# A one-core hybrid encoder step: other SBUF addresses for matmul operands, one block's down products summed over two chunks, and a wider last multiply

## The chip, the cores and the metric

The kernel runs on one core of a Trainium2 chip. The metric is the device time of one execution in microseconds (us). It is quoted as the median of several runs of the same program; one further execution was recorded by the hardware profiler, and all rows below come from that one.

## What is computed

One layer of a streaming encoder for 2048 prompt frames and 32 sample frames, model width 1024. The reference, cut to its steps:

```python
z = rmsnorm(h, g_attn) @ w_in                  # q, k, v of two head groups
oa = diff_attn(qa, ka, va, t5_table, lam)      # 4 heads, two softmax maps each
ob = band_attn(qb, kb, vb, band_table)         # 8 heads, a band of 9 chunks of 64
h = h + concat(subnorm(oa), rmsnorm(ob)) @ w_out
c = rmsnorm(h, g_mlp)
h = h + square(relu(c @ w_up)) @ w_down        # 1024 -> 4096 -> 1024
h = h + sigmoid(h @ w_ple_gate) * (p @ w_ple_proj)
y = rmsnorm(h, g_final)
```

The outputs are y and the new keys and values of both groups, for the prompt and for the sample.

## The kernel before, in words

**Matmuls.** Every fp32 product is made of three fp32r matmuls (mm3, lines 220 to 222): each operand is split into a high part (a rounding copy, on ACT or DVE, line 182 or 184) and a low part (raw minus high, on POOL, lines 167 and 177, or on DVE, line 188). Of a matmul, the *stationary* operand (128 columns) is loaded into the array and the *moving* operand (up to 512 columns) streams past it. A row `ups<-cs,piece 128x256` is a matmul into PSUM tile `ups` with moving operand `cs`, stationary operand `piece`, and 256 moving columns.

**Blocks and stages.** The 2080 frames are four blocks: 0, 1 and 2 of 512 columns, and 3 of 544 (512 prompt and 32 sample frames), which is worked in two sub-blocks of 272 (SUBS, line 36). The stages, in order of time: norm and projections (`vps` values, `qps` queries and keys), in between and after them attention B (`sb`, `tpb`, `ob`) and attention A (`s` scores, `tpp` transposes, `o` output sums), output projections (`ops`), MLP (`ups` up products, `dps` down products), the gate (`gps`, `pps`), and the final norm. A scheduler that works from a timeline model of its own decides in which order the instructions of overlapping stages stand in each engine's queue. Each engine works through its queue in order; all DMAs are issued from SP's queue.

**The MLP of blocks 2 and 3 (mlp7, line 1170).** 16 chunks of 256 hidden units. In each chunk a Strassen-like scheme with seven products of half size replaces eight: seven `prod` calls (line 1198) of 12 matmuls each, 84 `ups` matmuls of 256 columns (block 2) or 272 (block 3). ACT copies (line 1202) and DVE adds (line 1204) empty their PSUM banks, and relu, square and split (lines 1207 to 1210) make two hidden tiles in high and low parts: four tiles `uh`, `ul` in the pool `uh` (`up` in the code), a ring of 20 tiles of 544 columns. The chunk's down products, `downs` (line 1174), run beside the next chunk's up products: 8 groups of 6 matmuls, and after each group one DVE add of the PSUM bank to the residual `h` (line 1193). Weights come in `wr` tiles by DMA and are split into `piece` tiles, a ring of 8 (six slots in pool `wp4`, two in `wx`). While block 2 is in this stage, `cstage` (line 1024) prepares the seven operands of block 3: it draws its `ct` and `cst` tiles from the same ring of 20, stores them to DRAM, and their slots come free when the store has landed.

**Addresses.** A tile lies at the same byte address in each of the 128 partitions. The matter of the change is where a matmul's moving operand starts, taken modulo 256 bytes; it is called the *phase* below. It follows from the tile widths. A tile of 512 or 1024 fp32 columns is a whole number of 256-byte steps; a ring tile of 544 columns is 2176 bytes, 8.5 steps, so that the tiles of that ring start at phase 0 and 128 in turn. The two sub-blocks of 272 columns lie 1088 bytes apart, so that the second starts 64 further on. Pools on the right side of SBUF are stacked below each other, so that what the first of them, `edge` (24 columns, 96 bytes), takes shifts all the others.

**The final norm (final, line 1368).** For block 3 (`end`), per sub-block: DVE makes the reciprocal root (lines 1401 to 1403) and scales h tile 7 (line 1405); tiles 6 and 5 are multiplied by it on POOL, tiles 4 to 0 by five DVE multiplies (line 1413), and each half of the eight tiles is stored by one DMA.

Of the kernel before, what the change touches and what calls it, by code (L numbers as in the profile page):

```python
# [20 lines left out]
P = 128  # L21
# [121 lines left out]


class Kern:
    def __init__(self, tc, a):
        self.tc = tc
        self.nc = tc.nc
        self.a = a
        self.nt = 3  # L150
        self.pieces = None

    def dma(self, dst, src):
# [36 lines left out]
    def wunit(self, src, shape, hi_eng="act", lo_eng="pool", pool=None):  # L190
        nc = self.nc
        if pool is None:
            raw = self.rawp.tile([P] + shape, F32, bufs=2, name="wr")
        else:
            raw = pool.tile([P] + shape, F32, tag="wr0", bufs=4, name="wr0")
        self.dma(raw, src)
        if self.pieces is not None:
            n = shape[0] // 2
            parts = []
            for x in range(2):  # L200
                parts.append(self.piece([n] + shape[1:]))
# [407 lines left out]
    def attn_a_pair(self, g, j, ka, ba, pool, ps_s, ps_t, ps_o, late, first=None):  # L609
# [72 lines left out]
        for c0 in range(0, len(kts), 4):  # L682
# [8 lines left out]
            else:  # L691
# [104 lines left out]
    def attn_b_pair(self, h, j, kt, v, kb, bb, q, t1, pool, ps_s, ps_t, ps_o, step, late):  # L796
# [9 lines left out]
        for qi, t in enumerate(tiles):  # L806
# [37 lines left out]
            def second(qi=qi, nr=nr, kts=kts, held=held, end=t is tiles[-1]):  # L844
                if qi == 0:
                    px.append(pool.tile([P, 6, 2, 256], F32R, tag="p", bufs=2, name="pb"))
                p = px[0]
                e = held[0]
# [65 lines left out]
    def oload(self, b, wk, up, out, r=None):  # L914
# [74 lines left out]
    def cparts(self, b, wk, cs, out, r):  # L989
# [34 lines left out]
    def cstage(self, b, up, out, r):  # L1024
# [6 lines left out]
        def parts(k, *which):  # L1031
            for x, raw in which:
                t = up.tile([P, up.aw], F32R, tag="u", name="cst")[:, :n]
                self.split(t[:, :m], t[:, m:], raw, "act", "dve")
# [3 lines left out]
        for k in range(4):  # L1038
            c = []
            for i in range(2):  # L1040
                tmp = up.tile([P, up.aw], F32, tag="u", name="ct")[:, :n]
                kk = k + 4 * i
# [127 lines left out]
    def mlp7(self, b, hh, box, ops, wk, up, mm, md):  # L1170
        nc = self.nc
        n = BN[b]
        m = n // 2
        def downs(ch, us):
            for dh in range(2):
                wh, wl = self.wunit(self.a["w_down"][2 * ch + dh], [2, 512])
                for d in range(4):
                    for s0, sn in SUBS[b]:
# [75 lines left out]
        for ch in range(DFF // (2 * P)):  # L1254
            if ch > 0:
                w = {}
                drain(weights(ch, w, self.piece))
            us = []
            for f in range(2):
                us.append([up.tile([P, up.aw], F32R, tag="u", name=x)[:, :n] for x in ("uh", "ul")])  # L1260
            r0, r1 = tmp("r0", n), tmp("r1", n)
# [12 lines left out]
            prod(c12, u2, w["s4"], "b22")  # L1274
            square(us[0], r0, "dve")
            next(prev, None)
            prod(c21, u3, w["a22"], "t4")
            square(us[1], r1, "pool")
            drain(prev)
            prev = downs(ch, us)  # L1280
            yield
        drain(prev)

    def hparts(self, b, wk, up, out):
        n, t0 = BN[b], 512 * b
        hH, hL = [[up.tile([P, BLK], F32R, tag="u", name="hu")[:, :n] for k in range(8)] for _ in range(2)]
        out.append((hH, hL))
# [7 lines left out]
    def ptile(self, b, up, wk):  # L1295
        n, t0 = BN[b], 512 * b
        pT = [[up.tile([P, up.aw], F32R, tag="u", name="pT") for _ in range(2)] for _ in range(2)]
        for k in range(2):
            raw = (
                up.tile([P, up.aw], F32, tag="u", name="praw") if wk is None  # L1300
                else wk.tile([P, BLK], F32, tag="tmp", bufs=self.nt, name="praw")
# [5 lines left out]
    def gate(self, b, h, up, act, md, wk=None, made=None, pT=None):  # L1307
# [13 lines left out]
        else:  # L1321
            hH, hL = [[up.tile([P, BLK], F32R, tag="u", name="hu")[:, :n] for k in range(8)] for _ in range(2)]
        if made is None:
            for k in range(8):
                self.split(hH[k], hL[k], h[:, k, :n], "act", "dve" if k % 2 else "pool")
        for dq in range(2):
            ph, pl = self.wunit(a["w_ple_proj"][dq], [2, 512])
            for d4 in range(4):
                d = 4 * dq + d4
                wh, wl = self.wunit(a["w_ple_gate"][d], [8, P])  # L1330
                for s0, sn in SUBS[b]:
# [5 lines left out]
                    sg = (  # L1337
                        up.tile([P, up.aw], F32, tag="u", name="sig") if wk is None
                        else wk.tile([P, BLK], F32, tag="tmp", bufs=self.nt, name="sig")
# [28 lines left out]
    def final(self, b, h, wk, mm):  # L1368
# [22 lines left out]
        for s0, sn in SUBS[b]:  # L1391
# [14 lines left out]
            for k in range(6, -1, -1):  # L1406
                hv = h[:, k, sub]
                if not end:
                    nc.vector.scalar_tensor_tensor(hv, hv, self.g_final[:, k : k + 1], y, op0=ALU.mult, op1=ALU.mult)  # L1409
                elif k in (5, 6):  # L1410
                    self.pool_tt(hv, hv, y, ALU.mult)
                else:
                    nc.vector.tensor_tensor(hv, hv, y, op=ALU.mult)
# [296 lines left out]
```

## Time and profile before

| what | us |
|---|---|
| median of 3 runs | 3025.55 (3023.77 to 3027.49) |
| the profiled execution, its own time | 3025.88 |
| its span, first to last instruction | 3023.8 |
| PE busy (matmuls, their ends modelled) | 2925.0 (97% of the span) |
| DVE, ACT, POOL busy | 1823.2, 1746.1, 1887.1 (60%, 58%, 62%) |
| mean granted TensorE clock | 0.990 of full speed |

Of the profiled execution's time, 2.1 us lie outside its span. The views used are: the page with its summary and its line of 40 slices; the list of waits (engine, line, what it waited for, us in total, times, longest); groups by line and shape (busy us, mean ns of one, idle time before); busy time by windows; and the timeline, whose rows give start, duration, engine, line and instruction. A matmul's duration holds its way through the array, which overlaps the next one's: what a matmul costs in a stream is the distance from start to start, its *pitch*.

### The profile page before, as it was taken

What the parts mean: (1) busy time and instruction counts of PE and PEld (TensorE: products, weight loads), DVE (VectorE), ACT (ScalarE), POOL (GpSimd) and SP (SyncE); (2) the same over time, 40 slices, a digit from 0 to 9 for tenths busy, and PEclk for the clock granted to TensorE, in tenths of its full rate; (3) what the DMA queues carried; (4) which work ended last, traced back from release to release, by engine and by line L of the source; (5) the groups of instructions that cost most, each with busy time, mean ns of one, the idle gap of its engine ahead of it and who ended that gap; (6) DMA issues with size and microseconds to landing.
All of it is one profiled execution on the core that took longest, in us unless ns stands there. A gap on an engine that the chain in (4) does not pass through costs nothing. (4 is left out here: it accounts for less than half of the span.)

```text
span 3023.8 us, 49919 instructions
## 1 busy us (share of the span) xinstructions
PE 2925.0 (97%) x17217; PEld 2576.6 (85%) x17217; DVE 1823.2 (60%) x4217; ACT 1746.1 (58%) x3226; POOL 1887.1 (62%) x2509
## 2 busy tenths in 40 slices
PE   8999999999989999999999999999999999999997
PEld 6798889999877888888888888778788887999997
DVE  5256554676565554667566566445677885677664
ACT  5365554777666665655665655554655455555455
POOL 2568775323465444666655655787688888787774
PEclk9999999999999999999999999999999999999999
DMA  9877867987887453655643543446423446323231
GB/s 311 283 235 237 242 205 220 272 238 223 251 251 219 136 152 105 188 150 168 207 143 124 149 141 111 157 157 209 162 91 134 142 142 239 129 91 119 98 103 54
DMA packets 295204, 528.45 MB, mean 175 GB/s; under 512 B 36316, under 2 KB 159232, under 8 KB 294952
## 3 DMA queue, kind: packets, MB, share of 16 engines
q1 hardware_dynamic: 294952, 525.27, 55.7%
q8 instruction: 136, 2.23, 0.3%
q14 instruction: 116, 0.95, 0.1%
HBM read 424.66 MB, written 104.45 MB: 175 GB/s over the span
## 5 line engine op out<-in xcount | busy, mean ns | idle before, releaser
L177 POOL TENSOR_TENSOR wl<-wr,wh 128x256 fp32r<-128x256 f32 x632 | 472.0, 780 | 246.2 <-ACT wh L182 218.3
L182 ACT ACTIVATE piece<-wr 128x512 fp32r<-128x512 f32 x406 | 245.4, 624 | 290.4 <-PE ups L221 131.2
L177 POOL TENSOR_TENSOR piece<-wr,piece 128x256 fp32r<-128x256 f32 x404 | 338.2, 862 | 93.5 <-ACT piece L182 87.0
L182 ACT ACTIVATE wh<-wr 128x1024 fp32r<-128x1024 f32 x228 | 240.0, 1055 | 200.2 <-PE ups L221 42.6
L167 POOL TENSOR_TENSOR wl<-wr,wh 128x256 fp32r<-128x256 f32 x280 | 216.6, 805 | 202.1 <-ACT wh L182 199.9
L220 PE MATMUL dps<-uh,piece 128*128 128x272 f32 (+1 forms) x768 | 246.7, 325 | 10.3 <-ACT piece L182 6.8
L167 POOL TENSOR_TENSOR piece<-wr,piece 128x256 fp32r<-128x256 f32 x280 | 237.2, 879 | 18.2 <-ACT piece L182 14.9
L222 PE MATMUL dps<-uh,piece 128*128 128x272 f32 (+1 forms) x768 | 247.1, 324 | 1.5 <-POOL piece L167 1.0
L221 PE MATMUL dps<-ul,piece 128*128 128x272 f32 (+1 forms) x768 | 247.0, 323 | 0.1
L221 PE MATMUL ups<-cs,piece 128*128 128x256 f32 (+1 forms) x864 | 244.8, 283 | 0.0
L220 PE MATMUL ups<-cs,piece 128*128 128x256 f32 (+1 forms) x864 | 244.8, 283 | 0.0
L222 PE MATMUL ups<-cs,piece 128*128 128x256 f32 (+1 forms) x864 | 244.7, 284 | 0.0
L220 PE MATMUL qps<-aH,wh 128*128 128x512 f32 (+1 forms) x640 | 227.4, 356 | 5.8 <-DVE ql L502 4.2
L221 PE MATMUL qps<-aL,wh 128*128 128x512 f32 (+1 forms) x640 | 227.2, 355 | 0.0
L222 PE MATMUL qps<-aH,wl 128*128 128x512 f32 (+1 forms) x640 | 226.7, 355 | 0.0
L665 ACT ACTIVATE e<-e,nm 128x128 f32<-128x128 f32 (+16 forms) x136 | 157.2, 1156 | 109.6 <-DVE nm L663 109.1
L1150 DVE TENSOR_TENSOR h<-h,dps 128x512 f32<-128x512 f32 x256 | 173.1, 681 | 69.0 <-PE dps L222 67.8
L1193 DVE TENSOR_TENSOR h<-h,dps 128x272 f32<-128x272 f32 (+1 forms) x384 | 188.8, 513 | 42.3 <-PE dps L222 41.7
L220 PE MATMUL dps<-uh,wh 128*128 128x512 f32 x512 | 204.7, 400 | 5.6 <-DVE h L1150 4.5
L220 PE MATMUL ups<-cH,wh 128*128 128x512 f32 x512 | 202.5, 396 | 0.0
L222 PE MATMUL ups<-cH,wl 128*128 128x512 f32 x512 | 202.3, 395 | 0.0
L221 PE MATMUL ups<-cL,wh 128*128 128x512 f32 x512 | 202.2, 395 | 0.0
(312 smaller groups left out, 9139.7 us busy)
## 6 DMA issues: line engine op xcount, KB each, us to landing
wr<-w_up SPq DMA_DIRECT2D x128, 512.0 KB, 3.5
wr<-w_down SPq DMA_DIRECT2D x128, 512.0 KB, 3.5
q<-qS SPq DMA_DIRECT2D x128, 256.0 KB, 5.2
v<-vSa SPq DMA_DIRECT2D x64, 512.0 KB, 4.6
wr<-w_qk SPq DMA_DIRECT2D x50, 512.0 KB, 5.0
ka<-kS SPq DMA_DIRECT2D x32, 512.0 KB, 7.4
wr<-w_out SPq DMA_DIRECT2D x32, 512.0 KB, 4.5
wr<-w_ple_gate SPq DMA_DIRECT2D x32, 512.0 KB, 4.1
```

Of the source, the lines that this page charges most:

```text
L167: nc.gpsimd.tensor_tensor(out[:, sl], a[:, sl], b[:, sl], op=op)
L177: nc.gpsimd.tensor_tensor(out[:, sl], a[:, sl], b[:, sl], op=op)
L182: nc.scalar.activation(hi, raw, AF.Copy)
L220: nc.tensor.matmul(ps, lh, rh, start=start and i == 0, stop=False)
L221: nc.tensor.matmul(ps, lh, rl, start=False, stop=False)
L222: nc.tensor.matmul(ps, ll, rh, start=False, stop=stop and i == n - 1)
L665: nc.scalar.activation(row, row, AF.Exp, bias=nmx, accum_out=z[:nr, m : m + 1])
L1150: nc.vector.tensor_tensor(hv, hv, ps, op=ALU.add)
L1193: nc.vector.tensor_tensor(hv, hv, ps, op=ALU.add)
```

## The change

**1. Addresses.** The ring of 20 becomes `Even`: every tile takes 576 columns (2304 bytes, 9 steps of 256), and one of more than 512 columns starts 32 columns (128 bytes) into it. `wh`/`wl` tiles get 1152 columns and, for the value weights (shape 4 x 256, which are moving operands of `vps`), start 48 columns (192 bytes) in. `pH`/`pL` of attention A and `p` of attention B get spacer tiles ahead and behind. `edge` grows from 24 to 56 columns, which shifts all pools on the right by 128 bytes, and `cs` starts 48 instead of 16 columns in, which keeps its operands for block 2 where they were. A spacer of 120 columns moves the first value weights. In phases of moving operands, worked out from the tiles' addresses:

| moving operand (columns) | matmuls | phase before | phase after |
|---|---|---|---|
| ring of 20 in dps, gps, pps, ops (512) | 1440 | 0 and 128 | 0 |
| ring of 20 in dps, pps (272) | 1632 | 0, 64, 128, 192 | 128, 192 |
| wh, wl in vps (256) | 1248 | 0 | 192 |
| first value weights in vps (512) | 192 | 96 | 0 |
| pH, pL in o (256) | 768 | 128 | 192 |
| ka in s (512; 384; 256) | 400; 112; 96 | 0 and 128 | 0 |
| cs in ups (256) | 1296 | 192 | 192 |
| cs in ups (272) | 1296 | 0, 64, 128, 192 | the same |
| cH, cL in ups and aH, aL in qps (512) | 2688 | 0 | 0 |

Of stationary operands, the `piece` tiles in `wx` go from phase 128 to 0, attention A's `v` and transposed `e` from 128 to 0, and attention B's `q` and `e` from 0 to 128.

**2. Down products of block 2.** `downs` is called for two chunks at once: 8 groups of 12 matmuls per two chunks in place of 16 groups of 6, and 64 DVE adds in place of 128. The first of five `next(prev)` steps of a chunk pair now splits two weight units at once, and the hidden tiles of two chunks stay in the ring until the second following chunk. Block 3 is as before.

**3. Last norm.** For block 3 tiles 5 and 4 go to POOL, 6 to DVE, and tiles 3 to 0 are multiplied in one DVE instruction of 4 x 272 columns.

The order of the queues also changes where no line of the code was moved. Three places follow, before and then after; the names are those of the rows above.

On PE, in the first 100 us: queries and keys (`qps`) of the first blocks, and where the first attention scores (`s`) stand. Before:

```order
L222 MATMUL qps<-aH,wl 128x512
L650 MATMUL s<-ka,q 128x128 x4
L220 MATMUL qps<-aH,wh 128x512
L221 MATMUL qps<-aL,wh 128x512
L222 MATMUL qps<-aH,wl 128x512
```

After:

```order
L241 MATMUL qps<-aH,wl 128x512
L669 MATMUL s<-ka,q 128x128 x4
L239 MATMUL vps<-wh,aH 128x256
L240 MATMUL vps<-wl,aH 128x256
L241 MATMUL vps<-wh,aL 128x256
```

The first scores stood 216 `qps` matmuls into an unbroken run of them, with 120 more behind; they now stand behind an unbroken run of 357, at the first value products of the next group. Up to about 500 us the queues differ in many such places; from there to the last output projections they hold the same order.

On PE, in block 2's MLP: `ups` and `dps` of one chunk. Before, a group of six:

```order
L222 MATMUL ups<-cs,piece 128x256
L220 MATMUL dps<-uh,piece 128x512
L221 MATMUL dps<-ul,piece 128x512
L222 MATMUL dps<-uh,piece 128x512
L220 MATMUL dps<-uh,piece 128x512
L221 MATMUL dps<-ul,piece 128x512
L222 MATMUL dps<-uh,piece 128x512
L220 MATMUL ups<-cs,piece 128x256
```

After, at the first groups of a chunk pair:

```order
L241 MATMUL dps<-uh,piece 128x512
L239 MATMUL dps<-uh,piece 128x512
L240 MATMUL dps<-ul,piece 128x512
L239 MATMUL ups<-cs,piece 128x256
L240 MATMUL ups<-cs,piece 128x256
L241 MATMUL ups<-cs,piece 128x256
L239 MATMUL dps<-uh,piece 128x512
L240 MATMUL dps<-ul,piece 128x512
L241 MATMUL dps<-uh,piece 128x512
L239 MATMUL dps<-uh,piece 128x512
L240 MATMUL dps<-ul,piece 128x512
L241 MATMUL dps<-uh,piece 128x512 x2
```

A group of six stood between up products; now a group of twelve is opened, set aside for up products, and taken up again, and the second weight unit's groups are begun beside the first's. The other groups of a pair stand in unbroken twelves.

On ACT, late in block 2's MLP, with what each row waits for (DMAHW is a DMA's landing): `cst` are operands of block 3, `piece` weights, `t` a copy out of PSUM. Before:

```order
L182 ACTIVATE cst<-ct 128x272 x2
L182 ACTIVATE cst<-ct 128x272 [waits DMAHW0_49]
L182 ACTIVATE piece<-wr 128x512 [waits DMAHW4_49,PE_49]
L182 ACTIVATE piece<-wr 128x512 [waits PE_49]
L1202 ACTIVATE t_27647<-ups 128x256 [waits PE_49]
```

After:

```order
L196 ACTIVATE piece<-wr 128x512 [waits PE_49,Pool_49]
L196 ACTIVATE cst<-ct 128x272 [waits DMAHW6_49]
L196 ACTIVATE cst<-ct 128x272
L196 ACTIVATE cst<-ct 128x272 [waits DMAHW0_49]
L196 ACTIVATE piece<-wr 128x512 [waits PE_49]
```

In this stage 6 rows that write `cst` or `uh` waited for a DMA; now 10 do.

The diff, cut to its core (the remaining ring tiles change as the `oact` and `us` lines do):

```diff
+class Even:
+    whole = False
+
+    def __init__(self, pool, aw):
+        self.pool, self.aw = pool, aw
+
+    def tile(self, shape, dt, tag, name):
+        w = shape[1]
+        t = self.pool.tile([P, 576], dt, tag=tag, name=name)
+        o = 32 if w > 512 else 0
+        return t[:, o : o + w]
...
-            hi = self.wp.tile([P] + shape, F32R, tag="wh", bufs=3, name="wh")
-            lo = self.wp.tile([P] + shape, F32R, tag="wl", bufs=3, name="wl")
+            o = 48 if shape == [4, 256] else 0
+            hi, lo = [
+                self.wp.tile([P, 1152], F32R, tag=x, bufs=3, name=x)[:, o : o + 1024].rearrange(
+                    "p (k c) -> p k c", c=shape[1]
+                )
+                for x in ("wh", "wl")
+            ]
...
+            fresh = pool is not self.spaced
+            if fresh:
+                self.spaced = pool
+                pool.tile([P, 48], F32, tag="gap0", bufs=1, name="gap")
             pH = pool.tile([P, 4, 256], F32R, tag="pH", bufs=2, name="pH")
             pL = pool.tile([P, 4, 256], F32R, tag="pL", bufs=2, name="pL")
+            if fresh:
+                pool.tile([P, 80], F32, tag="gap1", bufs=1, name="gap")
...
-            oact = [[up.tile([P, up.aw], F32R, tag="u", name="ou")[:, :n] for k in range(8)] for _ in range(2)]
+            oact = [[up.tile([P, n], F32R, tag="u", name="ou") for k in range(8)] for _ in range(2)]
...
-            ops[x] = [t[:, 16 : 16 + 4 * m].rearrange("p (k c) -> p k c", c=m) for t in tiles]
+            ops[x] = [t[:, 48 : 48 + 4 * m].rearrange("p (k c) -> p k c", c=m) for t in tiles]
...
+        double = int(b == 2)
+
         def downs(ch, us):
             for dh in range(2):
-                wh, wl = self.wunit(self.a["w_down"][2 * ch + dh], [2, 512])
+                w = [self.wunit(self.a["w_down"][2 * (ch + c) + dh], [2, 512]) for c in range(len(us) // 2)]
...
-                                    wh[:, f, P * d : P * d + P],
-                                    wl[:, f, P * d : P * d + P],
+                                    w[f // 2][0][:, f % 2, P * d : P * d + P],
+                                    w[f // 2][1][:, f % 2, P * d : P * d + P],
...
-                                for f in range(2)
+                                for f in range(len(us))
...
-            us = []
+            if ch % 2 == 0 or not double:
+                us = []
             for f in range(2):
-                us.append([up.tile([P, up.aw], F32R, tag="u", name=x)[:, :n] for x in ("uh", "ul")])
+                us.append([up.tile([P, n], F32R, tag="u", name=x) for x in ("uh", "ul")])
...
-            square(us[0], r0, "dve")
+            square(us[-2], r0, "dve")
...
-            square(us[1], r1, "pool")
-            drain(prev)
-            prev = downs(ch, us)
+            square(us[-1], r1, "pool")
+            if ch % 2 or not double:
+                drain(prev)
+                prev = downs(ch - double, us)
...
-                elif k in (5, 6):
+                elif k in (4, 5):
                     self.pool_tt(hv, hv, y, ALU.mult)
-                else:
+                elif k == 6:
                     nc.vector.tensor_tensor(hv, hv, y, op=ALU.mult)
+                elif k == 0:
+                    hv = h[:, :4, sub]
+                    nc.vector.tensor_tensor(hv, hv, y.unsqueeze(1).broadcast_to((P, 4, sn)), op=ALU.mult)
...
-            opened(top, "edge", 1, side="right").tile([P, 24], F32, name="edge")
+            opened(top, "edge", 1, side="right").tile([P, 56], F32, name="edge")
...
+                pp.tile([P, 120], F32, tag="gap", bufs=1, name="gap")
...
-            up = Sized(opened(top, "uh", 20, side="right"), BLK)
+            up = Even(opened(top, "uh", 20, side="right"), BLK)
```

More of the change, by code (lines that the diff above doesn't have):

```diff
@@ L151, in __init__ @@
         self.pieces = None
+        self.spaced = None
     def dma(self, dst, src):
@@ L845, in second @@
                 if qi == 0:
+                    fresh = pool is not self.spaced
+                    if fresh:
+                        self.spaced = pool
+                        pool.tile([P, 96], F32, tag="gap0", bufs=1, name="gap")
                     px.append(pool.tile([P, 6, 2, 256], F32R, tag="p", bufs=2, name="pb"))
+                    if fresh:
+                        pool.tile([P, 32], F32, tag="gap1", bufs=1, name="gap")
                 p = px[0]
@@ L1032, in parts @@
             for x, raw in which:
-                t = up.tile([P, up.aw], F32R, tag="u", name="cst")[:, :n]
+                t = up.tile([P, n], F32R, tag="u", name="cst")
                 self.split(t[:, :m], t[:, m:], raw, "act", "dve")
@@ L1040, in cstage @@
             for i in range(2):
-                tmp = up.tile([P, up.aw], F32, tag="u", name="ct")[:, :n]
+                tmp = up.tile([P, n], F32, tag="u", name="ct")
                 kk = k + 4 * i
@@ L1285, in hparts @@
         n, t0 = BN[b], 512 * b
-        hH, hL = [[up.tile([P, BLK], F32R, tag="u", name="hu")[:, :n] for k in range(8)] for _ in range(2)]
+        hH, hL = [[up.tile([P, n], F32R, tag="u", name="hu") for k in range(8)] for _ in range(2)]
         out.append((hH, hL))
@@ L1296, in ptile @@
         n, t0 = BN[b], 512 * b
-        pT = [[up.tile([P, up.aw], F32R, tag="u", name="pT") for _ in range(2)] for _ in range(2)]
+        pT = [[up.tile([P, n], F32R, tag="u", name="pT") for _ in range(2)] for _ in range(2)]
         for k in range(2):
             raw = (
-                up.tile([P, up.aw], F32, tag="u", name="praw") if wk is None
+                up.tile([P, n], F32, tag="u", name="praw") if wk is None
                 else wk.tile([P, BLK], F32, tag="tmp", bufs=self.nt, name="praw")
@@ L1321, in gate @@
         else:
-            hH, hL = [[up.tile([P, BLK], F32R, tag="u", name="hu")[:, :n] for k in range(8)] for _ in range(2)]
+            hH, hL = [[up.tile([P, n], F32R, tag="u", name="hu") for k in range(8)] for _ in range(2)]
         if made is None:
@@ L1337, in gate @@
                     sg = (
-                        up.tile([P, up.aw], F32, tag="u", name="sig") if wk is None
+                        up.tile([P, sn], F32, tag="u", name="sig") if wk is None
                         else wk.tile([P, BLK], F32, tag="tmp", bufs=self.nt, name="sig")
```

## The prediction, made before the changed kernel ran

> **What bounds the kernel.** I read the page's summary and slices first, then the list of PE's waits, then PE's timeline in stretches without waits.
>
> ```profile
> PE 2925.0 (97%) x17217; PEld 2576.6 (85%) x17217; DVE 1823.2 (60%) x4217; ACT 1746.1 (58%) x3226; POOL 1887.1 (62%) x2509
> ...
> PE   8999999999989999999999999999999999999997
> ```
>
> PE is busy nine tenths or more in all but three slices of forty, and no other engine is near it over the whole. So the time is PE's: the sum of its pitches, plus its waits. The longest waits, of the whole kernel and then of block 2's MLP (2170 to 2530 us), where the down products change:
>
> ```profile
> PE vps L220 <- ACT wh L182: 8.9, 1, 8.9
> PE dps L220 <- ACT piece L182: 6.8, 6, 1.6
> ...
> PE gps L220 <- ACT piece L182: 5.6, 2, 5.4
> ```
> ```profile
> PE dps L220 <- ACT piece L182: 6.8, 6, 1.6
> PE dps L220 <- DVE h L1193: 1.6, 1, 1.6
> PE dps L222 <- POOL piece L167: 1.0, 3, 0.7
> PE dps L220 <- ACT uh L182: 0.6, 1, 0.6
> ```
>
> No wait costs 10 us in all, and block 2's four come to 10.0 us. What is saved on a matmul's pitch therefore reaches the end of the kernel nearly whole; what is saved on DVE, ACT or POOL does not, except through these waits.
>
> **Addresses, 256 columns.** Four streams of 256 columns, first and last row of each. Attention A's output sums, moving operand at phase 128 (24 matmuls, so 23 pitches):
>
> ```profile
> 1310.31 0.28 PE L723 MATMUL o<-pH,v 128*128 128x256 f32 x1
> ...
> 1313.07 0.28 PE L725 MATMUL o<-pH,v 128*128 128x256 f32 x1
> ```
>
> Value products at phase 0 (35 matmuls):
>
> ```profile
> 365.73 0.28 PE L220 MATMUL vps<-wh,aH 128*128 128x256 f32 x1
> ...
> 369.81 0.28 PE L222 MATMUL vps<-wh,aL 128*128 128x256 f32 x1
> ```
>
> Block 2's up products at phase 192, one stream of 123 and one of 36:
>
> ```profile
> 2174.49 0.28 PE L220 MATMUL ups<-cs,lead 128*128 128x256 f32 x1
> ...
> 2188.32 0.28 PE L222 MATMUL ups<-cs,piece 128*128 128x256 f32 x1
> ...
> 2247.54 0.28 PE L220 MATMUL ups<-cs,piece 128*128 128x256 f32 x1
> ...
> 2251.66 0.28 PE L222 MATMUL ups<-cs,piece 128*128 128x256 f32 x1
> ```
>
> The pitches are 2.76/23 = 120.0 ns, 4.08/34 = 120.0, 13.83/122 = 113.4 and 4.12/35 = 117.7 ns. All these stretches are free of waits, so the difference is in the matmul itself; phases 128 and 0 cost the same in two stages with different work beside them, while phase 192 has a fast and a less fast kind. I take their middle, 115.5. The change puts 768 `o` and 1248 `vps` matmuls on phase 192: 2016 x (120.0 - 115.5) = 9.1 us. Since some values stand in short runs between scores, I take 8.2. Bounds: nothing, if the phase is not the cause, and 2016 x 6.6 = 13.3 us.
>
> **Addresses, 512 columns.** Phase 0 (34 up products of block 0), then phase 96 (71 first value products), then the old ring with its phases 0 and 128 in turn (24 gate products, and 44 down products of block 2):
>
> ```profile
> 1199.31 0.40 PE L221 MATMUL ups<-cL,wh 128*128 128x512 f32 x1
> ...
> 1206.82 0.39 PE L221 MATMUL ups<-cL,wh 128*128 128x512 f32 x1
> ```
> ```profile
> 39.93 0.40 PE L221 MATMUL vps<-wl,aH 128*128 128x512 f32 x1
> ...
> 56.27 0.39 PE L222 MATMUL vps<-wh,aL 128*128 128x512 f32 x1
> ```
> ```profile
> 2113.88 0.39 PE L220 MATMUL gps<-hu,piece 128*128 128x512 f32 x1
> ...
> 2119.24 0.39 PE L222 MATMUL gps<-hu,piece 128*128 128x512 f32 x1
> ```
> ```profile
> 2514.22 0.39 PE L222 MATMUL dps<-uh,piece 128*128 128x512 f32 x1
> ...
> 2524.14 0.39 PE L222 MATMUL dps<-uh,piece 128*128 128x512 f32 x1
> ```
>
> The pitches are 7.51/33 = 227.6 ns, 16.34/70 = 233.4, 5.36/23 = 233.0 and 9.92/43 = 230.7 ns. The old ring loses about 231.9 - 227.6 = 4.3 ns. Its stage is also the one where the other engines are busiest, so that not all of it need be the phase; I take 2.4 ns on 1440 matmuls, 3.4 us (bounds 0 and 5.4 x 1440 = 7.8). The first value products gain 5.8 x 192 = 1.1 us (bounds 0 and 1.1). Of the 608 score matmuls on `ka` half stood at phase 128; at the same 2.4 ns that is 304 x 2.4 = 0.7 us (bounds 0 and 304 x 5.8 = 1.8).
>
> **Addresses without a price of their own.** For the 1632 matmuls of 272 columns and the moved stationary operands no stretch of one phase alone stands in the trace. The nearest difference is that of the two streams at phase 192, 4.3 ns; 1632 x 4.3 = 7.0 us either way would be the far end, but 272 columns leave half of the old phases in place, so I take 0 and keep 2 us either way. Sum of the addresses: 8.2 + 3.4 + 1.1 + 0.7 = **13.4 us**, bounds about -2 and 26.
>
> A rule of the Trainium skill speaks against this whole part. "TensorE: Matmul & The Clock Gate", section "Wait — 56ns, not 53.3ns?", gives the warm start-to-start time as N / 2.4 GHz plus about 2.5 ns, with no word of addresses. By that, 256 columns would take 109.2 ns and 512 columns 215.8 ns wherever they lie, and this part would be worth 0. The trace does not agree: it shows 113.4 to 120.0 and 227.6 to 233.4 ns, all above the rule and different by stream.
>
> **Block 2's down products.** No matmul is added or removed. 64 of 128 DVE adds go:
>
> ```profile
> L1193 DVE TENSOR_TENSOR h<-h,dps 128x512 f32<-128x512 f32 x128 | 83.8, 676 | 1.9 <-PE dps L222 1.9
> L1193 DVE TENSOR_TENSOR h<-h,dps 128x272 f32<-128x272 f32 x256 | 105.0, 432 | 40.5 <-PE dps L222 39.8
> ```
> ```profile
> core 0: us, PE busy (x) PEld busy (x) DVE busy (x) ACT busy (x) POOL busy (x), PEclk, DMA share, GB/s
> ...
> 2320.00:2390.00 70.00, 64.66 (x406) 57.32 (x405) 59.88 (x87) 33.12 (x65) 55.30 (x59) 1.00 0.47 159
> 2390.00:2460.00 70.00, 67.72 (x416) 59.20 (x415) 58.25 (x87) 35.44 (x69) 58.51 (x65) 1.00 0.45 150
> ```
>
> That is 64 x 676 ns = 43.3 us of DVE, which runs beside PE: hidden but for the waits quoted above. DVE at 59 of 70 us is the busiest engine beside PE here, and it stands behind the 6.8 us on `piece`, since ACT's splits wait for DVE's sums of weights. At best all 10.0 us go. On the other side, two weight units are now split at the start of a pair, and up to 16 of 20 ring tiles are held. So four more ACT rows wait for a store (10 in place of 6), and behind them stand weight splits and the copies out of PSUM on which PE's up products wait; on SP the `ct` loads wait for ring slots with weight loads behind them. A store takes
>
> ```profile
> cSt<-cst SPq DMA_DIRECT2D x16, 272.0 KB, 4.1
> ```
>
> so these waits are 4 x 4.1 = 16.4 us of ACT, which has 35 us idle in every 70. I take 2 us gained (between 10 gained and 16 lost), since the scheduler has fewer first groups to starve and ACT has room.
>
> **The last norm.** Its rows are the end of the kernel, so here DVE is the path:
>
> ```profile
> 3011.50 1.92 POOL L167 TENSOR_TENSOR h<-h,ry 128x272 f32<-128x272 f32 x2 [17.91 <-DVE ry L1403]
> ...
> 3011.81 2.97 DVE L1413 TENSOR_TENSOR h<-h,ry 128x272 f32<-128x272 f32 x5
> ```
>
> Five multiplies take 2.97 us, 0.59 each. A wide one is not in the trace; from the two rows of adds above a column costs (676 - 432)/240 = 1.02 ns and an instruction 155 ns at its start, so an estimate for 4 x 272 columns is 155 + 1088 x 1.02 = 1.26 us, against four at 0.43 to 0.59: 1.7 to 2.4 us. Per sub-block 0.5 to 1.1 us, but POOL's two multiplies end the first half later: I take 0.5, so 1.0 us in all (bounds 0 and 2.2).
>
> **The moved order of the first 500 us** adds and removes no work. What it can do is bring or remove one wait of the kind that also costs clock: after a wait of 3 us the granted clock of a stretch falls,
>
> ```profile
> PE qps L220 <- DVE ql L502: 4.2, 2, 3.0
> ```
> ```profile
> 90.00:135.00 45.00, 42.02 (x176) 34.28 (x175) 7.02 (x19) 13.39 (x26) 21.30 (x31) 0.92 0.99 300
> ```
>
> 3.0 us of wait and 45 x 0.08 = 3.6 us of clock, 6.6 us either way. I take 0.
>
> **Sum**, against the profiled execution's 3025.88 us (0.33 above the median of 3025.55): 3025.9 - 13.4 - 2.0 - 1.0 = 3009.5; I say **3010**.
>
> **Rivals.** *The phase is not the cause* (the rule's result): the streams differ by what runs beside them. For it: the old ring's slow streams stand where the other engines are busiest. Against: `o` and `vps` have the same 120.0 ns in different company. It leaves 3025.9 - 3.0 = 3023. *Only 512 columns pay*: phase 192 inherits its kind from the stream ahead (113.4 and 117.7 under one phase), and between scores it falls back to 118 to 120. Then 8.2 us are missing: 3018. *Block 2's ring runs dry, and the kernel is slower*: each of the 10 rows that wait for a store holds ACT for 4.1 us, the copies behind it keep PSUM banks, and PE waits as long: 41 us lost, less 16.4 gained, 3050. It decides from (16.4 + 6)/10 = 2.2 us per row. Against it: ACT's idle time, and PE has other blocks' products only at the stage's ends, which is for it.
>
> **Chances.** Forecast 0.63 (3001 to 3018 with the order's 6.6 us either way), only 512 pay 0.15, phase not the cause 0.14, ring dry 0.08. A measurement of this kernel tells a change of about 0.2% (6 us) from none. Faster by more: 0.62 of the forecast and 0.10 of the second, 0.72; within 0.2%: 0.20 (the rest of those two and the third); slower 0.08. The range takes in the second and third cases and, below, the 256-column bound: 2999 to 3025.
>
> **What would show it.** Right: `o` and `vps` streams at 113 to 118 ns; `gps` and block 2's `dps` near 228; 64 rows of the 512-column add at 0.68 us; PE's waits in block 2 under 10 us; two wide multiplies of about 1.3 us at the end. Wrong: streams that keep their pitch, or waits of `ups` on ACT's copies in block 2, with `cst` rows waiting for DMAs.

## The result and the profile after

The changed kernel takes 3008.91 us (median of 5, 3002.77 to 3015.24), the kernel before 3026.31 us (median of 5). The ratio is 0.9947, with a 95% interval of 0.9933 to 0.9962: 16.0 us faster by the ratio, between 11.5 and 20.3. A second series gave 3006.59 against 3025.61 us, 0.9941 (0.9929 to 0.9953). The forecast was 3010 us.

The profiled execution of the changed kernel took 3002.77 us, the shortest of its five. Its span is 3001.0 us, 22.8 shorter than before, and some 6 us of that are luck of this one execution: its mean granted clock was 0.993, that of the other four 0.989 to 0.991. Its summary and slices:

```profile
PE 2903.3 (97%) x17217; PEld 2567.9 (86%) x17217; DVE 1798.7 (60%) x4147; ACT 1743.6 (58%) x3226; POOL 1877.2 (63%) x2509
## 2 busy tenths in 40 slices
PE   8999999999989999999999999999899999999997
```

The same 17217 matmuls, 21.7 us less of PE busy: PE still bounds the kernel, and its matmuls have become shorter. The streams that answer to those of before, first and last row of each. Attention A's output sums, two streams of 24, one behind down products and one behind a score of 384 columns:

```profile
1300.23 0.28 PE L748 MATMUL o<-pH,v 128*128 128x256 f32 x1
...
1302.94 0.28 PE L750 MATMUL o<-pH,v 128*128 128x256 f32 x1
...
1369.71 0.28 PE L748 MATMUL o<-pH,v 128*128 128x256 f32 x1
...
1372.35 0.28 PE L750 MATMUL o<-pH,v 128*128 128x256 f32 x1
```

The pitches are 2.71/23 = 117.8 and 2.64/23 = 114.8 ns, against 120.0 before. Value products (26 in a row):

```profile
445.06 0.28 PE L239 MATMUL vps<-wh,aH 128*128 128x256 f32 x1
...
447.90 0.28 PE L240 MATMUL vps<-wl,aH 128*128 128x256 f32 x1
```

2.84/25 = 113.6 ns, against 120.0. Then the ring of 20 at phase 0: block 2's last 96 down products, and 34 gate products:

```profile
2481.12 0.39 PE L239 MATMUL dps<-uh,piece 128*128 128x512 f32 x1
...
2502.65 0.39 PE L241 MATMUL dps<-uh,piece 128*128 128x512 f32 x1
...
2514.21 0.39 PE L239 MATMUL gps<-hu,piece 128*128 128x512 f32 x1
...
2521.69 0.39 PE L241 MATMUL gps<-hu,piece 128*128 128x512 f32 x1
```

21.53/95 = 226.6 ns and 7.48/33 = 226.7 ns, against 230.7 and 233.0. But block 2's up products, whose phase was left at 192, became slower (168 in a row):

```profile
2159.03 0.28 PE L239 MATMUL ups<-cs,lead 128*128 128x256 f32 x1
...
2178.70 0.28 PE L241 MATMUL ups<-cs,piece 128*128 128x256 f32 x1
```

19.67/167 = 117.8 ns, where the first stream of before had 113.4. That was in no step of the forecast.

PE's waits in block 2's MLP (2159 to 2502.7 us); before, four kinds came to 10.0 us. Below them is ACT's wait for stores in the same stretch, which the kernel before didn't have:

```profile
PE dps L241 <- POOL piece L181: 3.5, 4, 2.0
PE dps L239 <- ACT piece L196: 2.6, 2, 2.2
```
```profile
ACT piece L196 <- DMA cSt<-cst: 7.5, 2, 3.8
```

And the window in which PE had waited 3.0 us for `ql` and the granted clock had fallen to 0.92:

```profile
90.00:135.00 45.00, 43.21 (x192) 35.45 (x191) 10.73 (x25) 15.92 (x37) 22.41 (x33) 1.00 0.98 331
```

**Where the time went, from all pairs of neighbouring matmuls of one shape in both traces** (mean pitch before and after, times the number of matmuls; where one stops calling a distance a pitch moves each term by 0.1 to 0.3 us):

| term | forecast, us | measured, us |
|---|---|---|
| `vps` 118.9 to 115.4 ns, `o` 119.4 to 116.8 ns | -8.2 | -6.3 |
| ring of 20, 512 columns: 231.2 to 227.2 ns | -3.4 | -5.8 |
| first `vps`, 512 columns: 233.4 to 228.3 ns | -1.1 | -1.0 |
| scores on `ka` | -0.7 | -0.4 |
| `dps` of 272 columns: 125.4 to 124.9 ns | 0 (2 either way) | -0.8 |
| block 2's `ups`: 115.4 to 117.5 ns | none | +2.7 |
| all addresses | -13.4 | -11.6 |
| block 2's MLP, by its length | -2.0 | -6.0, of it -5.7 the down products (below) |
| last norm | -1.0 | -0.2 |

### The profile page after: what moved, and what is told of

The parts are those of the page before. It is cut to its first block, busy times and chain, and to the rows that moved or that the text cites. A ratio compares the mean times of both kernels' runs of the same rounds, so it can differ in the third digit from the quotient of the medians.

```text
span 3001.0 us, 49834 instructions
## 1 busy us (share of the span) xinstructions
PE 2903.3 (97%) x17217; PEld 2567.9 (86%) x17217; DVE 1798.7 (60%) x4147; ACT 1743.6 (58%) x3226; POOL 1877.2 (63%) x2509
## 5 line engine op out<-in xcount | busy, mean ns | idle before, releaser
L196 ACT ACTIVATE piece<-wr 128x512 fp32r<-128x512 f32 x406 | 247.2, 625 | 268.9 <-PE ups L240 123.3
L241 PE MATMUL dps<-uh,wl 128*128 128x512 f32 x512 | 200.8, 392 | 0.0
```

The lines of the kernel that those rows point to most:

```text
L196: nc.scalar.activation(hi, raw, AF.Copy)
L241: nc.tensor.matmul(ps, ll, rh, start=False, stop=stop and i == n - 1)
```

## The experiments

Four questions were open. Is the phase the cause, or the company? Which part brought how much? Why did block 2's up products slow down? And what in the doubled down products shortened block 2?

**Streams alone (e1_pitch).** The kernel is replaced by streams of one kind, each of 96 matmuls or, where the last number says so, of 48. `PH` holds the phases 0, 32 to 224; `m[q]` is a moving operand at phase q, `w[q]` a stationary one:

```diff
+                for q in PH:
+                    self.stream(b[o], m[q], 256, 256, w[0])
...
+                for q in PH:
+                    self.stream(b[o + 2], m[q], 512, 512, w[0], 48)
...
+                for q in (0, 128, 192):
+                    self.stream(b[o + 1], m[q], 256, 256, w[128])
```

> Leaves out the whole computation: only streams of matmuls from eight copies of one operand, which start 0, 32, ... 224 bytes into a step of 256, first with the other engines idle, then with DVE, ACT and POOL busy. Theory A, the phase sets the pitch: 256 columns take about 120 ns at phases 0 and 128 and 113 to 118 at 192, 512 columns about 227 at 0, 231 at 128 and 233 at 96, and the busy half repeats the idle half within 1 ns. Theory B, what runs beside sets it: all phases have one pitch in the idle half, near 113 and 227 ns, and the busy half is slower by 3 to 6 ns.

Windows that hold one stream each (length, then the busy time of PE, PEld, DVE, ACT, POOL, the clock, DMA). First 256 columns with the stationary operand at phase 0, moving phases 0, 128, 192; then with the stationary operand at 128, moving phases 128 and 192; then 48 matmuls of 512 columns: moving and stationary phase 0/0, 128/0, 0/128, 128/128.

```profile
46.02:57.52 11.50, 11.50 (x97) 11.50 (x96) 0.00 (x0) 0.00 (x0) 0.00 (x0) 1.00 0.00 0
91.65:103.04 11.39, 11.39 (x98) 11.39 (x97) 0.00 (x0) 0.00 (x0) 0.00 (x0) 1.00 0.00 0
114.31:125.22 10.91, 10.91 (x99) 10.91 (x97) 0.00 (x0) 0.00 (x0) 0.00 (x0) 1.00 0.01 2
...
375.75:387.26 11.51, 11.51 (x98) 11.51 (x97) 0.00 (x0) 0.00 (x0) 0.00 (x0) 1.00 0.01 1
387.26:398.57 11.31, 11.31 (x98) 11.31 (x97) 0.00 (x0) 0.00 (x0) 0.00 (x0) 1.00 0.01 1
...
227.05:237.95 10.90, 10.90 (x50) 9.02 (x49) 0.00 (x0) 0.00 (x0) 0.00 (x0) 1.00 0.00 0
...
271.37:282.56 11.19, 11.19 (x49) 9.01 (x48) 0.00 (x0) 0.00 (x0) 0.00 (x0) 1.00 0.01 1
...
398.57:409.72 11.15, 11.15 (x50) 9.05 (x49) 0.00 (x0) 0.00 (x0) 0.00 (x0) 1.00 0.00 0
409.72:420.66 10.94, 10.94 (x50) 9.01 (x49) 0.00 (x0) 0.00 (x0) 0.00 (x0) 1.00 0.01 1
```

The lengths over 96 are 119.8, 118.6 and 113.6 ns; with the stationary operand at 128 they are 119.9 and 117.8. The lengths over 48 are 227.1, 233.1, 232.3 and 227.9 ns. So the moving phase alone doesn't decide: 128 is good for 512 columns if the stationary operand stands at 128 too, and 192 is good for 256 columns only if it stands at 0. It is the **distance between the two phases** that counts (moving minus stationary, modulo 256 bytes). And the busy half, with DVE, ACT and POOL at work (256 columns at 0 and 192, 512 columns at 0):

```profile
423.45:434.95 11.50, 11.50 (x97) 11.50 (x96) 10.99 (x12) 10.08 (x16) 9.17 (x9) 1.00 0.00 0
491.74:502.65 10.91, 10.91 (x98) 10.91 (x97) 10.57 (x11) 10.40 (x17) 10.91 (x10) 1.00 0.01 2
604.48:615.39 10.91, 10.91 (x51) 9.01 (x49) 10.59 (x10) 10.40 (x17) 10.91 (x11) 1.00 0.00 0
```

To 0.01 us the same lengths. Theory B, the company, is out for DVE, ACT and POOL; DMA stood nearly still in both halves (a share of 0.03 at most) and isn't tested. Theory A holds with the distance in place of the phase.

**Addresses alone (e2_addr).** The changed kernel with two parts undone:

```diff
-        double = int(b == 2)
+        double = 0
...
-                elif k in (4, 5):
+                elif k in (5, 6):
...
```

> The changed kernel with the down products of block 2 and the last norm as before, so addresses alone. If the addresses carry the change, as forecast: 13.4 us faster than the kernel before, 3010 to 3015 us. If the pitch of streams is only half of it and the doubled down products the rest: 6 to 9 us faster.

3013.82 against 3022.86 us, ratio 0.9971 (0.9960 to 0.9982): 8.8 us, between 5.4 and 12.1. The forecast's 13.4 us lie outside that interval; the second expectation, 6 to 9 us, fits. Its pitches are those of the changed kernel, 11.6 us less than before.

**The other two parts alone (e3_double).** The kernel before with the new `downs` and the new last multiply.

> The kernel before with the doubled down products and the wide last multiply, and no address moved on purpose. Forecast terms: 2 us and 1 us faster, 3021 to 3024 us. By the trace of the changed kernel, whose block 2 is 6 us shorter at nearly equal pitches: 5 to 7 us faster, 3019 to 3021 us, and nothing at the end.

3017.63 against 3022.86 us, ratio 0.9975 (0.9962 to 0.9989): 7.6 us, between 3.3 and 11.5. The two ratios multiply to 0.9946, the whole change's 0.9947: the parts add up within their intervals. Between executions of one kernel there are up to 18 us (before: 3016.04 to 3033.97 in 29), so that for a single part the length of its stage tells more. Block 2's MLP, first `ups` to last `dps`, in the kernel before, the addresses alone, and the other two parts alone:

```profile
2174.49:2524.14 349.65, 339.03 (x2118) 300.17 (x2117) 269.94 (x404) 184.70 (x355) 286.41 (x328) 1.00 0.43 146
```
```profile
2168.53:2518.23 349.70, 340.21 (x2118) 304.02 (x2117) 270.21 (x404) 184.99 (x355) 284.94 (x328) 1.00 0.43 146
```
```profile
2162.48:2506.45 343.97, 337.99 (x2119) 301.99 (x2118) 239.60 (x345) 187.82 (x360) 283.41 (x330) 0.99 0.45 155
```

The doubled down products are worth 5.7 us there, with the old addresses. The addresses are worth nothing in this stage: what the ring's `dps` gain, the `ups` lose.

**Only 256 columns (e4_256).** The kernel before with the new place of `wh`/`wl` and with `pH`/`pL` 64 bytes further, so that `vps` and `o` stand at 192 and nothing else has moved.

> The kernel before with only the 256-column operands moved: value weights from phase 0 to 192 and attention A's exponentials from 128 to 192. Phase theory, by the forecast's price: 8.2 us faster, 3016 to 3019 us; by the pitches of the changed kernel's trace (3.6 ns on 1248 and 2.6 ns on 768) 6.5 us faster. If only 512 columns pay: within 2 us of before.

3023.75 against 3022.86 us, ratio 1.0002 (0.9989 to 1.0015): between 3.3 us faster and 4.5 slower. The pitches did fall, `vps` from 118.9 to 115.8 and `o` from 119.4 to 117.7 ns, 5.2 us in all. The time doesn't show it: 5.2 us faster lies outside the interval. Where a pitch saved ahead of a wait goes is taken up below. One more sign of the distance: attention A's `v`, the stationary operand of `o`, still stood at phase 128 here, so that `o` had distance 64, which takes 117.8 ns in the streams alone. All 14 long streams of `o` in this trace lie at 117.7 to 118.0 ns; in the changed kernel, at distance 192, twelve lie at 117.8 and two at 113.7.

**What stands ahead of a stream (e5_entry).** Streams in the MLP's order, high and low parts as in mm3. `ups` makes 36 matmuls of 256 columns at phase q, `downs` 12 of 512 columns with the phases of the high and the low part:

```diff
+                for _ in range(3):
+                    self.ups(b[0], q)
+                    self.downs(b[1], 0, 0)
...
+                    self.downs(b[3], 0, 128)
```

> Leaves out the whole computation: streams of matmuls alone, in the order that the MLP has them (high and low parts, three matmuls a term), 36 of 256 columns and 12 of 512 in turn, the other engines idle. First the 256 columns at 16 phases with the 512 at phase 0, then with high parts at 0 and low parts at 128 as in the ring before, then the same with a third of the weights at phase 128, then 512 and 272 columns at 16 phases. Theory A, only the distance of the moving from the stationary operand's phase counts: 256 columns at distance 192 take 113.5 ns whatever stands ahead of them. Theory B, a stream keeps a state that the stream ahead of it has set: at distance 192 it takes 117.8 ns behind 512 columns at phase 0 and 113 to 116 behind phases 0 and 128 in turn.

Streams of 36: phase 192 behind 512 columns at phase 0; phase 112 behind the same; phase 192 behind 0 and 128 in turn; the same with a third of the weights at 128 (the page of this run has no ACT, so that the third busy time is DVE's and the fourth POOL's):

```profile
299.71:303.95 4.24, 4.24 (x38) 4.24 (x36) 0.00 (x0) 0.00 (x0) 1.00 0.00 0
194.78:198.90 4.12, 4.12 (x37) 4.12 (x36) 0.00 (x0) 0.00 (x0) 1.00 0.02 4
447.03:451.14 4.11, 4.11 (x38) 4.10 (x36) 0.00 (x0) 0.00 (x0) 1.00 0.00 0
530.71:534.82 4.11, 4.11 (x38) 4.10 (x36) 0.00 (x0) 0.00 (x0) 1.00 0.01 4
```

117.8, 114.4, 114.2 and 114.2 ns. The same operands at the same distance take 117.8 ns in every matmul of the stream, or 113.4 from the sixth on, and the stream ahead decides which. Theory B holds: this is the slowdown of `ups`. With the ring all at phase 0, the down products settle at 226.7 ns and hand the up products the slow state; with the ring's two phases they were irregular, and the up products mostly fell into the fast one.

**The piece slots (e7_wx128, e8_wx0).** In the changed kernel, `wx` is pushed back to phase 128; in the kernel before, it alone is moved to 0:

```diff
+            opened(top, "gap0", 1, side="right").tile([P, 32], F32, name="gap")
             wx = opened(top, "wx", 2, side="right")
...
+            opened(top, "gap1", 1, side="right").tile([P, 32], F32, name="gap")
```

> The changed kernel with the two piece slots of wx back at phase 128, every other address as changed. Distance theory (moving phase minus stationary phase decides): the 256-column up products of block 2, of which a quarter then stand at distance 64, stay at 117.5 ns or fall to 114 to 116 if the state from the stream ahead is broken up; the ring's 512 columns rise from 227 to 228 to 229 ns, since a quarter stands at distance 128. Moving phase alone: both keep 117.5 and 227 ns.

> The kernel before with only the two piece slots of wx moved from phase 128 to 0; moving operands stay. If the stationary operands are what slowed the up products of block 2: 117.5 ns in place of 115.4. If the ring's phases, in the stream ahead, did it: 113.5 to 115.5. The ring's 512 columns, half at distance 0 and half at 128: 230 to 231 ns.

In block 2's MLP the first has `ups` at 116.2 ns (changed kernel: 117.5) and `dps` at 230.3 (227.6), more than the forecast 228 to 229: a quarter of the matmuls at the 233.1 ns of distance 128 would make 229.0 (an estimate), so others must have slowed too. No moving operand stands elsewhere, so the moving phase alone is out in the kernel too. The second has `ups` at 114.9 (115.4 before) and `dps` at 231.1 (231.1): the stationary operands didn't slow the up products, the ring's new phase did.

**DVE's adds (e6_dummy, e10_half).** Two tries to part the 64 adds saved from the groups of twelve. The first takes the kernel of e3_double and adds DVE work; the second takes the kernel before and leaves out the adds of every second chunk, so that half of block 2's sum is missing:

```diff
+                            nc.vector.tensor_tensor(scr, hv, hv, op=ALU.add)
...
+                        if b != 2 or ch % 2 == 0:
                             nc.vector.tensor_tensor(hv, hv, ps, op=ALU.add)
```

> The kernel before with the doubled down products and the wide last multiply, and behind each of the 64 adds of block 2 a second add of 512 columns on DVE into a scratch tile that nobody reads: the groups of twelve stay, the DVE time comes back. If fewer DVE adds are what made block 2's MLP 5.7 us shorter: it is back at 348 to 350 us. If it is the groups of twelve and the order of the weights: it stays at 343 to 345 us.

> The kernel before, but the down products of every second chunk of block 2 are not added to the residual (half of that block's sum is left out): 64 DVE adds less, groups of six and the order of the weights as before. If fewer DVE adds shorten block 2's MLP: 349.65 us fall to 341 to 345, as with the doubled down products or more. If the groups of twelve do it: 348 to 350.

```profile
2172.86:2538.00 365.14, 344.24 (x2118) 304.38 (x2117) 287.14 (x405) 186.86 (x360) 300.54 (x327) 0.98 0.42 143
```
```profile
2172.72:2521.44 348.72, 340.54 (x2119) 301.25 (x2118) 238.16 (x345) 187.15 (x357) 283.53 (x327) 1.00 0.43 146
```

The first went outside both expectations, 365.1 us, and doesn't tell them apart: the adds out of SBUF were longer than those out of PSUM, and POOL's work stretched to 300.5 us:

```profile
L1198 DVE TENSOR_TENSOR scr<-h 128x512 f32<-128x512 f32 x59 | 54.5, 924 | 0.7
L1195 DVE TENSOR_TENSOR h<-h,dps 128x512 f32<-128x512 f32 x63 | 41.8, 676 | 4.2 <-PE dps L222 4.2
```

The second is clean: DVE has 31.8 us less to do (e3_double: 30.3), and the stage is 0.9 us shorter, not 5.7. So fewer adds by themselves are not the cause. PE's waits in it:

```profile
PE dps L220 <- ACT piece L182: 4.0, 6, 1.0
PE dps L220 <- DVE h L1194: 1.9, 1, 1.9
PE dps L222 <- POOL piece L167: 1.5, 7, 0.4
```

It still waits six times for `piece` on ACT, as the kernel before does; the changed kernel does so twice. Counted over the stage, PE stands for more than 150 ns between an up product and the first down product behind it 14 times before, 12 times in this run and 5 times in the changed kernel. What went away are the places where a group of down products is begun. That grouping by itself, at the old DVE load, would keep the 5.7 us isn't shown: the one run for it was overloaded.

**Phase 112 (e9_cs112, e11_all112), and the changed kernel again (after_again).** The first of two tries to go further moves only block 2's operands, the second also `vps` and `o`:

```diff
-            ops[x] = [t[:, 48 : 48 + 4 * m].rearrange("p (k c) -> p k c", c=m) for t in tiles]
+            ops[x] = [t[:, 28 : 28 + 4 * m].rearrange("p (k c) -> p k c", c=m) for t in tiles]
...
-            o = 48 if shape == [4, 256] else 0
+            o = 28 if shape == [4, 256] else 0
```

> The changed kernel with block 2's 256-column operands 28 columns into their tiles in place of 48: phase 112 in place of 192, nothing else moved. If the streams alone tell it (36 matmuls behind 512 columns at phase 0: 117.79 ns at 192, 114.44 at 112): the up products go from 117.5 to 114 to 115 ns and the stage of block 2's MLP loses 3 to 4.5 us, so 3004 to 3006 us against some 3009 of the changed kernel. If the pitch hides a wait that then shows: pitch falls, the stage keeps its 343.6 us.

> As the run before it, and the value weights and attention A's exponentials also at phase 112. Their streams are short and stand between other kinds, so the price is open: if 112 is the better phase whatever stands ahead, vps falls from 115.4 and o from 116.8 ns to 113.5 to 114.5, together 3 to 4 us more; if it was good only behind 512 columns at phase 0, they stay or rise to 118.

> The changed kernel once more, beside the runs of this call, so that they are compared on one chip: 14 to 20 us faster than the kernel before, 11.6 of it in matmul pitches and some 6 in block 2's waits.

| kernel | median, us | ratio to before (95%) | `ups`, `dps` in block 2, ns | block 2's MLP, us |
|---|---|---|---|---|
| changed kernel again | 3006.59 | 0.9941 (0.9929 to 0.9953) | 117.6, 227.7 | 344.6 |
| cs at 112 | 3007.98 | 0.9946 (0.9933 to 0.9959) | 115.3, 228.9 | 343.3 |
| cs, vps and o at 112 | 3011.67 | 0.9953 (0.9937 to 0.9970) | 115.3, 228.8 | 344.8 |

The up products gain as the streams said, and the down products behind them lose 1.2 ns (in e5_entry twelve of them take 229.3 ns each behind phase 112 and 226.6 behind 192): of 3 us 2 are left, and the time doesn't show them. In the third kernel `vps` rose to 116.6 ns and `o` fell to 116.2. No version beats the changed kernel.

**What becomes of a saved pitch.** Six traces have the new addresses but for the one move tried (changed kernel twice, e2, e7, e9, e11), and five likewise the old (before, e3, e6, e8, e10). Their means by stage, old to new. The usual pitch is put at 227, 125 and 114 ns for 512, 272 and 256 columns and at 0.445 ns a column for other widths. A distance between two matmuls of over 150 ns above it counts as a wait. The pitch excess is what distances of up to 1.6 times the usual pitch have above it, for the three widths named. The last column is the time in which the trace grants TensorE half its clock:

| stage | length, us | waits, us | pitch excess, us | at half clock, us |
|---|---|---|---|---|
| first `vps` to first `sb` | 505.0 to 495.7 | 26.2 to 22.8 | 12.3 to 8.0 | 8.9 to 4.6 |
| to first `ops` | 276.7 to 278.6 | 10.4 to 11.6 | 5.9 to 4.8 | 0.7 to 5.7 |
| to last `o` | 1106.4 to 1108.1 | 33.0 to 37.4 | 26.2 to 23.6 | 11.6 to 17.1 |
| to block 2's first `ups` | 273.0 to 273.7 | 24.8 to 26.2 | 3.9 to 2.1 | 14.3 to 18.8 |
| block 3's MLP | 420.6 to 418.7 | 2.3 to 2.0 | 3.0 to 1.4 | 0 |

Of the first four stages only the first got shorter, by 9.3 us, and it is also the one whose queue was reordered. In e4_256 PE's queue holds the order of before through this stage, and its pitch excess there is already down to 9.0 us; yet the stage takes 507.0 us, with 32.3 us of waits (24.8 to 28.3 in the five, 20.6 to 25.2 in the six). So in the old order the shorter pitches ended as waits. It seems to be the new order that lets them count, but one trace tells it, and no run has the new order with the old addresses.

In the next three stages, the pitches fall by 1.1, 2.6 and 1.8 us and the stages get no shorter: the waits grow by 7.1 us in all, and distances of about twice the usual pitch by 2.8. Of these 9.9 us, 5.8 lie where the clock is halved: there 512 columns take 427 ns and 272 columns 227. The same 23 `qps` matmuls of 272 columns, at the same place of PE's queue behind the first band scores, in the changed kernel again and in e8_wx0 (the clock is the third number from the end):

```profile
512.07:517.45 5.38, 5.38 (x24) 5.38 (x25) 2.31 (x13) 3.96 (x11) 1.83 (x4) 0.50 0.69 183
```
```profile
520.86:523.88 3.02, 3.02 (x24) 3.02 (x25) 2.16 (x12) 2.51 (x9) 1.55 (x2) 1.00 0.65 186
```

In these traces the three stages have 41.5 us at half clock with the new addresses and 26.6 with the old. Over all executions the difference is smaller: the mean granted clock is 0.9905 in 29 of the kernel before and 0.9900 in 12 of e2_addr, which makes 1.5 us (an estimate: 0.0005 of 3020 us). So part of what these few traces show can be chance. Only block 3's MLP, which hardly waits and has no halved clock, keeps what its pitches gain.

## Why the prediction was right, and where it was not

**The bound** was right as far as PE has still 97% of its span. But that a saved pitch "reaches the end of the kernel nearly whole" was not: from the first `sb` to block 2's first `ups`, 5.5 us of pitch were saved and the stages became 4.3 us longer, and e4_256 saved 5.2 us of pitch and no time.

**256 columns**, 8.2 us forecast: `o` and `vps` gave 6.3, within the bounds. Phase 192 does have two kinds, and `o` shows both, 117.8 and 114.8 ns. But the step was built on the moving operand's phase, and it is the distance to the stationary operand that counts: `o` at 128 and `vps` at 0 had the same 120.0 ns because both had distance 0. That the stream ahead chooses the kind stood in a rival ("phase 192 inherits its kind") but in no term. With that the up products' 2.7 us of loss would have been on the list; "no stretch of one phase alone" was looked for, when the pairs were there to be sorted.

**512 columns**, 3.4 us forecast, 5.8 measured: the discount for the busy engines was wrong. The streams alone repeat to 0.01 us beside busy engines, so nothing had to be taken off for DVE, ACT and POOL. First value products (1.1, measured 1.0) and scores (0.7, measured 0.4) were right.

**The rule of N / 2.4 GHz plus 2.5 ns** ("TensorE: Matmul & The Clock Gate" of the Trainium skill, section "Wait — 56ns, not 53.3ns?"), which would have made this part worth 0, doesn't hold for these fp32r streams: no phase out of 16 gave a stream under 113.3 ns for 256 columns or 226.6 for 512, and the addresses move them up to 120.2 and 234.7; by the rule one would estimate 109.2 and 215.8.

**Block 2's down products** were mis-sized: 2 us forecast, 5.7 measured, inside the bounds of 10 gained and 16 lost. The mechanism named, fewer first groups to starve, fits the count of 14, 12 and 5; DVE's 43 us, which stood beside it, are by e10_half (31.8 us less on DVE) worth 0.9 us. The rival, the ring running dry, did not occur: ACT did wait for stores, 7.5 us where 16.4 were reckoned with, but PE's waits in block 2 name no `ups` waiting for ACT's copies.

**The last norm** gave 0.2 us of 1.0. The wide multiply, forecast at 1.26 us, on DVE, and POOL's two multiplies beside it:

```profile
2987.85 0.44 DVE L1437 TENSOR_TENSOR sqy<-sqy,ry 128x272 f32<-128x272 f32 x1
...
2989.22 1.00 DVE L1448 TENSOR_TENSOR h<-h,ry 128x272 f32<-128x272 f32 x1
2990.14 1.84 DVE L1451 TENSOR_TENSOR h<-h,ry 128x1088 f32<-128x1088 f32 x1
```
```profile
2988.94 1.89 POOL L181 TENSOR_TENSOR h<-h,ry 128x272 f32<-128x272 f32 x2 [17.99 <-DVE ry L1438]
```

1.84 us, with 1.00 for the single one ahead: 2.8 us where five took 2.97. The estimate came from adds that read PSUM. A multiply of 272 columns with all operands in SBUF takes 0.44 us before POOL starts (L1437) and 1.00 beside it (L1448); the forecast had no term for that.

**The order of the first 500 us** was put at 0, 6.6 either way. That is the term the sum was lucky with. The stage became 9.3 us shorter, 4.3 of it by pitches, 3.4 by waits and most of the rest by fewer distances at half clock; with the old order (e4_256) it stayed at 507.0 us. The prediction looked for a fallen clock only here; it came in the stages behind, and why the waits and the half-clock time grow there isn't settled.

**The sum** was right to about 1 us because errors cancelled, which is luck: the addresses gave 1.8 us less than forecast in pitches and still less in time (8.8 us in e2_addr, and that with the new order), the down products 3.7 more, the norm 0.8 less.

## What to carry to other kernels

Sort a trace's matmul pitches by the phases of both operands before changing an address, and price the streams behind the moved ones too, since they can change their state with nothing moved in them. A pitch saved in a stage with waits may come back as a wait or as time at half clock; count it in full only where PE doesn't wait, and look at the queue's order before crediting a stage's gain to its pitches. Where PE starves at the first matmul of each weight unit, fewer and longer groups may help (here they came with half of the adds gone), and taking work off the engine beside it need not.

## What was not expected of the hardware

With nothing but matmuls running, 256 columns took 113.3 to 120.2 ns, 512 columns 226.6 to 234.7 and 272 columns 123.3 to 126.7, by where the moving operand starts relative to the stationary one in steps of 16 bytes. 512 columns are best at distances 0 and 240 (227.2 and 226.9 ns), worst at 208 (234.6). At distance 192, 256 columns have two steady pitches, 113.4 and 117.8 ns, and keep the one they fall into through a whole stream (168 matmuls in the changed kernel). At 128, too, one and the same stream took 118.6 and 119.9 ns in e5_entry. Ahead of the final norm the granted clock falls to half for 3.4, 6.8 or 10.2 us at a time, and the same stretch of the queue meets it in one trace and not in another. An add of 512 columns on DVE took 676 ns with one operand in PSUM and 924 ns with both in SBUF, in the same stage of e6_dummy.
